# First output projection with the context's tiles first, and the context's expert products in three runs per expert

## The chip, the cores and the metric

The kernel runs on one core of one Trainium2 chip. The metric is the device time of one execution in microseconds, and times shown are medians of several executions. The engines are named as in the profile: PE (TensorE), DVE (VectorE), ACT (ScalarE), POOL (GpSimd) and SP (SyncE); 16 DMA engines move data between HBM and the chip's memories for all of them.

## The reference

Two layers on 1024 latents and 256 context tokens of 1024 features. Layer 0 mixes with a hyena convolution, layer 1 with sliding-window attention; both end in an expert-choice feed-forward (each expert picks its tokens). The context is dropped after layer 1's keys, so only layer 0 has experts on the context.

```python
D_MODEL, SEQ, CTX_LEN, N_EXPERTS, EXPERT_FF, EC_CAPACITY = 1024, 1024, 256, 16, 1024, 2

def expert_choice_ffn(h, router_w, w_gate, w_up, w_down):
    B, n, D = h.shape
    cap = EC_CAPACITY * n // N_EXPERTS            # 128 latents, 32 context tokens
    aff = jax.nn.softmax((h @ router_w).astype(F32), axis=-1)
    gate, idx = lax.top_k(jnp.swapaxes(aff, 1, 2), cap)
    xe = jax.vmap(lambda hb, ib: hb[ib])(h, idx)
    a = jnp.einsum('becd,edf->becf', xe, w_gate)
    u = jnp.einsum('becd,edf->becf', xe, w_up)
    ye = jnp.einsum('becf,efd->becd', jax.nn.silu(a) * u, w_down) * gate[..., None].astype(h.dtype)
    return jax.vmap(lambda ib, yb: jnp.zeros((n, D), h.dtype).at[ib.reshape(-1)].add(yb.reshape(-1, D)))(idx, ye)

for layer in range(2):
    ...
    lat = lat + mod_l[2] * y_l                     # y_l, y_c: the mixer's output projection
    h_l = rms_norm(lat, norm2_w[layer]) * (1.0 + mod_l[4]) + mod_l[3]
    lat = lat + mod_l[5] * expert_choice_ffn(h_l, moe_router[layer], moe_w_gate[layer], ...)
    if keep_ctx:                                   # layer 0 only
        cx = cx + mod_c[2] * y_c
        h_c = rms_norm(cx, norm2_w[layer]) * (1.0 + mod_c[4]) + mod_c[3]
        cx = cx + mod_c[5] * expert_choice_ffn(h_c, ...)
return rms_norm(lat, final_norm_w)
```

## The kernel before

The program is written with a tile framework: tiles come from pools with a fixed number of buffers, a scheduler orders the instructions of each engine by a priority that follows the order of the code (`high_priority` moves a block ahead, `issue_after` ties a block behind an instruction), and a tile's buffer is used again when all readers of the tile before have ended. All weight loads of the experts are issued by SP, whose queue is in order: a load that waits for its buffer holds up the loads behind it.

**The output projection** is the class `Mix`. Its method `stream` works on one tile of 128 tokens after the other: 48 products at L777 (each f32 product is three matmuls of high and low parts), DVE's residual and norm (L780 to L789), transposes of the normed tile (L795), the router (L799), a softmax, and one transpose of the affinities (L807) that `put_lat` (L1485) or `put_ctx` (L1488) copies into `affl` (48 x 512) or `affc` (16 x 256). In layer 0 `body` calls it for the eight latent tiles, then for the two context tiles, then issues the last eight of 24 pieces of the next layer's modulation (`a1.piece`, L66), and then searches: `route_lat` finds the 128 best latents of each expert with 16 rounds of max, index and replace on DVE (L819, L820, L822; `top_rows`), and `top_rows` on `affc` finds the 32 best context tokens in four rounds. The ids of the search start the gather of the first expert's rows (`xg`, L959, on POOL), and with it the expert stage.

**The expert stage** is `Moe.run`. An expert's weights are 12 tiles `raw` of 1 MB: (e, 0) to (e, 7) are 128 rows each of gate and up (L920, L921), (e, 8) to (e, 11) are 256 rows each of down (L923). There are nine buffers for them in layer 0, so the load of each tile waits for the release of the tile nine places earlier. Each tile is split into `whi` (ACT, L935) and `wlo` (DVE, L936), three buffers each. For the latents PE multiplies with gate and up at L981 (12 matmuls of 512 columns per `raw` tile, `gu(e, kk)`) and with down at L1039 (12 per tile). `gu(e+1, 0)` and `gu(e+1, 1)` are placed inside expert e, while the activation `g` of expert e is made and transposed (L950), so the code of expert e itself begins with `gu(e, 2)`. The result is scaled on DVE (L1053) and added to the stream in HBM by an indirect DMA (L1054, the scatter).

For the context's 32 tokens of an expert PE multiplies straight from `raw` in fp32, with four column groups of 32: `ctx_gu` (L966, 4 instructions per `raw` tile, `kk` 0 to 7) and `ctx_dn` (L973, 8 instructions per down tile). One such instruction is two records in the trace. A `raw` tile is free when ACT and DVE have split it and, in layer 0, the context's products have read it. Before the change `ctx_gu` comes in pairs of `kk`: (0, 1) at the start of expert e, (2, 3) after `gu(e, 3)`, (4, 5) after `gu(e, 5)`, (6, 7) after `gu(e+1, 0)`, and `ctx_dn` comes one down tile at a time behind the L1039 products of the tile after it. L1045 transposes the context's activation, L1059 and L1060 scale and scatter it.

## Time and profile before

| What | Before |
|---|---|
| Median of 3 runs | 3269.67 us (3264.92 to 3276.31) |
| Span of the profiled execution | 3265.9 us |
| PE busy | 3024.7 us (93%) |
| DVE busy | 2365.2 us (72%) |
| ACT busy | 1625.1 us (50%) |
| POOL busy | 554.8 us (17%) |
| DMA, bytes moved | 717.12 MB, mean 220 GB/s |
| Expert stage of layer 0, PE busy from 1224 to 2020 us | 791.12 of 796 us |
| Expert stage of layer 1, PE busy from 2670 to 3235 us | 558.94 of 565 us |

The profiled execution's own time is its span, 3265.9 us, which is 3.8 us under the median. Busy time of matmuls overlaps and its ends are modelled, so a price of a matmul is read from start to start of neighbours, not from its duration.

### The profile page before, as it was taken

How to read it: one execution, taken by the hardware profiler on the slowest of the kernel's cores; microseconds unless marked ns; L12 is line 12 of the kernel's file. 1: busy time of each engine (PE TensorE's matmuls, PEld its weight loads, DVE VectorE, ACT ScalarE, POOL GpSimd, SP SyncE). 2: the span in 40 equal slices, each digit the busy share in tenths (PEclk: the TensorE clock that was granted, in tenths of full speed). 3: DMA queues.
4: the chain of work that ended last, by engine and by line, in shares of the span. 5: the costliest groups of instructions: out<-in, count | busy, mean ns of one | idle time of the engine just before them, and what ended most of it. 6: DMA issues, size and time to landing. Idle time of an engine off the chain costs nothing. (4 is left out here: it accounts for less than half of the span.)

```text
span 3265.9 us, 43095 instructions
## 1 busy us (share of the span) xinstructions
PE 3024.7 (93%) x15902; PEld 2315.5 (71%) x15902; DVE 2365.2 (72%) x3089; ACT 1625.1 (50%) x2106; POOL 554.8 (17%) x560
## 2 busy tenths in 40 slices
PE   6888999999987969999999998998999949999995
PEld 3677888876766836666666665887887838888884
DVE  6888752389996675766766765846886579999996
ACT  5456333310003425555555554426886437777774
POOL 4663000044452121010010000000000011111110
PEclk9999999999998979999999999999999969999998
DMA  7743432176726457787787785536114359999995
GB/s 226 250 167 135 127 107 81 68 231 198 251 89 215 168 195 249 268 297 277 272 299 276 272 286 178 174 100 229 54 44 149 123 212 376 397 391 394 395 379 185
DMA packets 361652, 717.12 MB, mean 220 GB/s; under 512 B 45821, under 2 KB 201997, under 8 KB 354914
## 3 DMA queue, kind: packets, MB, share of 16 engines
q1 hardware_dynamic: 324792, 669.60, 56.8%
q0 software_dynamic: 12096, 37.75, 4.6%
q10 hardware_dynamic: 24554, 7.01, 1.0%
q8 instruction: 126, 2.06, 0.3%
q14 instruction: 84, 0.69, 0.1%
HBM read 603.64 MB, written 110.62 MB: 219 GB/s over the span
## 5 line engine op out<-in xcount | busy, mean ns | idle before, releaser
L936 DVE TENSOR_TENSOR wlo<-raw,whi 128x2048 fp32r<-128x2048 f32 x379 | 862.4, 2289 | 287.6 <-ACT whi L935 284.5
L935 ACT ACTIVATE whi<-raw 128x2048 fp32r<-128x2048 f32 x384 | 734.5, 1917 | 441.0 <-PE psA L981 226.8
L981 PE MATMUL psA<-wlo,xhi 128*128 128x512 f32 x1024 | 405.1, 396 | 0.8 <-DVE wlo L936 0.8
L981 PE MATMUL psA<-whi,xlo 128*128 128x512 f32 x1024 | 404.8, 396 | 0.0
L981 PE MATMUL psA<-whi,xhi 128*128 128x512 f32 x1024 | 387.8, 405 | 0.9 <-ACT xhi L33 0.9
L981 PEld LDWEIGHTS psA<-whi,xhi 128*128 128x128 f32 x1024 | 193.2, 189 | 84.3 <-issue 40.5
L981 PEld LDWEIGHTS psA<-wlo,xhi 128*128 128x128 f32 x1024 | 193.5, 189 | 52.0 <-issue 12.6
L981 PEld LDWEIGHTS psA<-whi,xlo 128*128 128x128 f32 x1024 | 193.1, 189 | 40.5
L1054 POOL DMA_INDIRECT lat_d<-ye,ids x32 | 77.3, 2415 | 778.4 <-DVE ye L1053 778.4
L411 PE MATMUL psA<-hThi,win_hi 128*128 128x512 f32 (+1 forms) x576 | 205.8, 358 | 0.0
L411 PE MATMUL psA<-hTlo,win_hi 128*128 128x512 f32 (+1 forms) x576 | 204.4, 355 | 1.2 <-DVE hTlo L34 1.2
L411 PE MATMUL psA<-hThi,win_lo 128*128 128x512 f32 (+1 forms) x576 | 203.9, 354 | 0.0
L1039 PE MATMUL psA<-whi,ghi 128*128 128x512 f32 x512 | 163.4, 400 | 1.1 <-ACT ghi L33 1.1
L1039 PE MATMUL psA<-wlo,ghi 128*128 128x512 f32 x512 | 160.0, 394 | 0.7 <-DVE wlo L936 0.7
L1039 PE MATMUL psA<-whi,glo 128*128 128x512 f32 x512 | 158.9, 391 | 1.2 <-DVE glo L34 1.2
L571 ACT ACTIVATE q<-psT 128x512 f32<-128x512 f32 x32 | 19.1, 597 | 266.4 <-PE psT L565 147.7
L157 PE MATMUL psT<-fleaf,tabF 128*128 128x256 f32 x512 | 125.6, 397 | 20.7 <-DVE fleaf L128 19.9
L966 PE MATMUL psC<-raw,xTc 128*32 128x512 f32 x1024 | 139.7, 599 | 0.0
L413 ACT ACTIVATE p<-psA,convw 128x512 f32<-128x512 f32 (+1 forms) x72 | 44.1, 612 | 176.4 <-PE psA L411 176.4
L777 PE MATMUL psA<-wo_hi,zhi 128*128 128x512 f32 x288 | 114.6, 402 | 15.5 <-ACT zhi L33 13.8
L157 PEld LDWEIGHTS psT<-fleaf,tabF 128*128 128x128 f32 x512 | 98.7, 199 | 41.9 <-issue 23.1
L959 POOL DMA_INDIRECT xg<-hl_d,ids x32 | 50.0, 1563 | 437.9 <-PE psT L950 387.1
(349 smaller groups left out, 6530.2 us busy)
## 6 DMA issues: line engine op xcount, KB each, us to landing
raw<-in_moe_w_gate_dram SPq DMA_DIRECT2D x256, 512.0 KB
raw<-in_moe_w_up_dram SPq DMA_DIRECT2D x256, 512.0 KB
raw<-in_moe_w_down_dram SPq DMA_DIRECT2D x128, 1024.0 KB
ada_wt<-in_ada_w_dram SPq DMA_DIRECT2D x48, 1024.0 KB
K_d<-kout SPq DMA_DIRECT2D x56, 256.0 KB
Kt<-K_d SPq DMA_DIRECT2D x112, 128.0 KB
win_raw<-in_hy_w_in_dram SPq DMA_DIRECT2D x24, 512.0 KB
lf_d<-lf SPq DMA_DIRECT2D x64, 128.0 KB
```

Source lines behind the costliest of these rows:

```text
L157: nc.tensor.matmul(ps[:, m, :], k.tabF[:, l, kin, m, :], x[:, kin, :], start=(kin == 0), stop=(kin == 1))
L411: nc.tensor.matmul(pt[:, :n], a[:, kk, :], b[:, kk, s:s + n], start=(i == 0), stop=(i == 23))
L413: nc.scalar.activation(p[:, dst:dst + n], pt[:, :n], AF.Identity, bias=cw[:, 0, c:c + 1])
L571: nc.scalar.activation(self.like(self.q), self.R[l], AF.Copy)
L777: nc.tensor.matmul(pt, a[:, kk, :], b[:, kk, hs], start=(kk == 0 and p == 0), stop=(kk == 7 and p == 2))
L935: nc.scalar.activation(whi, raw, AF.Copy)
L936: (engine or nc.vector).tensor_tensor(out=wlo, in0=raw, in1=whi.bitcast(F32), op=ALU.subtract)
L959: nc.gpsimd.indirect_dma_start(out=xg, out_offset=None, in_=h_d[0], in_offset=bass.IndirectOffsetOnAxis(ap=ids[:, e:e + 1], axis=0))
L966: nc.tensor.matmul(cgu[32 * q:32 * q + 32], xc[e // 4][:, kk, (e % 4) * 32:(e % 4) * 32 + 32], self.raw(e, kk)[:, :, q * 256:(q + 1) * 256 ...
L981: nc.tensor.matmul(acc[i], a[:, kk, :], b[:, i // 2, (i % 2) * 512:(i % 2) * 512 + 512], start=(kk == 0 and p == 0), stop=(kk == 7 and p = ...
L1039: nc.tensor.matmul(dn[i], a[:, kk, :], b[:, j, i * 512:i * 512 + 512], start=(kk == 0 and p == 0), stop=(kk == 7 and p == 2))
L1054: nc.gpsimd.indirect_dma_start(out=out_d[0], out_offset=bass.IndirectOffsetOnAxis(ap=ids[:, e:e + 1], axis=0), in_=y, in_offset=None, comp ...
```

## The change

In `body`, layer 0's `Mix` takes the context's two tiles first, then the context's search is written, then the eight latent tiles and their search, and last the eight modulation pieces. In `Moe.run` the context's products of an expert from 1 on stand in three runs: `ctx_gu` of `kk` 0 to 3 behind `gu(e, 4)`, `ctx_gu` of `kk` 4 to 7 behind `gu(e, 7)`, and all four down tiles of `ctx_dn` behind the L1039 products and the scatter. Expert 0's `ctx_gu` stands as one run ahead of its `gu`. The pools of PSUM get another rule for the waits of a reused buffer (`reuse_waits="tile"`). Comments of the code were dropped too; lines after L1015 have moved by 2 to 5 (L1039 is L1043 in the changed kernel, L1045 L1048, L1485 L1487).

```diff
@@ Moe.run
-                    nc.tensor.matmul(acc[i], a[:, kk, :], b[:, i // 2, (i % 2) * 512:(i % 2) * 512 + 512],
-                                     start=(kk == 0 and p == 0), stop=(kk == 7 and p == 2))
+                    last = nc.tensor.matmul(acc[i], a[:, kk, :], b[:, i // 2, (i % 2) * 512:(i % 2) * 512 + 512],
+                                            start=(kk == 0 and p == 0), stop=(kk == 7 and p == 2))
+            return last
...
+            cgu = k.psum.tile([128, 2, 256], F32, name="psC")
+            ctx_gu(0, cgu, range(8))
         acc = banks(4)
         for kk in range(2):
             gu(0, kk, acc, xT)
         for e in range(NE):
             nxt = gather(e + 1) if e + 1 < NE else None
-            cgu = k.psum.tile([128, 2, 256], F32, name="psC") if route_c else None
-            if route_c:
-                ctx_gu(e, cgu, (0, 1))
+            if route_c and e:
+                cgu = k.psum.tile([128, 2, 256], F32, name="psC")
             for kk in range(2, 8):
-                gu(e, kk, acc, xT)
-                if route_c and kk in (3, 5):
-                    ctx_gu(e, cgu, (kk - 1, kk))
+                last = gu(e, kk, acc, xT)
+                if route_c and e and kk == 4:
+                    with k.tc.issue_after(last.ins):
+                        ctx_gu(e, cgu, range(4))
...
+            if route_c and e:
+                with k.tc.issue_after(last.ins), k.tc.high_priority(offset=50):
+                    ctx_gu(e, cgu, range(4, 8))
...
-            if route_c:
-                ctx_gu(e, cgu, (6, 7))
...
-                if route_c:
-                    if k2 == 0:
...
-                    else:
-                        ctx_dn(e, cdn, cgT, k2 - 1)
+                if route_c and k2 == 0:
...
             if route_c:
-                ctx_dn(e, cdn, cgT, 3)
+                for k2 in range(4):
+                    ctx_dn(e, cdn, cgT, k2)
@@ Psum
-        self.pool = es.enter_context(tc.tile_pool(name=f"psum{Psum.n}", bufs=1, space=PSUM))
+        self.pool = es.enter_context(tc.tile_pool(name=f"psum{Psum.n}", bufs=1, space=PSUM, reuse_waits="tile"))
@@ body
-                      k.z2_d[:, :, :T])
+                      k.z2_d[:, :, T:])
+            mix.stream(1, 2, k.z2_d[:, :, T:], k.ctx, k.ctx_d, k.hc_d, put_ctx)
+            top_c = top_rows(k, affT[1], 32, rp, "c")
             mix.stream(0, 8, k.z2_d[:, :, :T], k.x, k.lat0_d, k.hl0_d, put_lat)
-            mix.stream(1, 2, k.z2_d[:, :, T:], k.ctx, k.ctx_d, k.hc_d, put_ctx)
+            route = route_lat(k, affT[0], rp)
             for i in range(16, 24):
                 a1.piece(i)
             rows1, cols1 = a1.rows, a1.cols
-            route = route_lat(k, affT[0], rp)
-            top_c = top_rows(k, affT[1], 32, rp, "c")
```

What the scheduler makes of it is seen in the order of each engine's instructions. The first place is PE inside expert 4 of layer 0 (`psC_10989` is the bank of its `ctx_gu`, `psC_11218` that of its `ctx_dn`; the numbered `raw` are its weight tiles in order of `kk`). Before, with the L981 and L1039 rows between left out, but for those beside the transposes of `g`:

```order
L966 MATMUL psC_10989<-raw_10807,xTc_9536 32x512 x4
L966 MATMUL psC_10989<-raw_10848,xTc_9536 32x512 x4
...
L966 MATMUL psC_10989<-raw_11000,xTc_9536 32x512 x4
L966 MATMUL psC_10989<-raw_11019,xTc_9536 32x512 x4
...
L966 MATMUL psC_10989<-raw_11101,xTc_9536 32x512
L950 MATMUL psT_11182<-ident_86,g_11144 128x128 x4
L966 MATMUL psC_10989<-raw_11101,xTc_9536 32x512 x3
L966 MATMUL psC_10989<-raw_11127,xTc_9536 32x512 x4
...
L973 MATMUL psC_11218<-raw_11223,cgT_11242 32x256 x8
...
L973 MATMUL psC_11218<-raw_11246,cgT_11242 32x256 x8
```

The same expert on PE in the changed kernel, with the same rows left out:

```order
L966 MATMUL psC_10989<-raw_10815,xTc_9536 32x512 x4
L966 MATMUL psC_10989<-raw_10848,xTc_9536 32x512 x4
L966 MATMUL psC_10989<-raw_10992,xTc_9536 32x512 x4
L966 MATMUL psC_10989<-raw_11011,xTc_9536 32x512 x4
L950 MATMUL psT_11065<-ident_86,xg_10987 128x128 x4
...
L966 MATMUL psC_10989<-raw_11030,xTc_9536 32x512 x4
L966 MATMUL psC_10989<-raw_11074,xTc_9536 32x512 x4
L966 MATMUL psC_10989<-raw_11093,xTc_9536 32x512 x4
L966 MATMUL psC_10989<-raw_11119,xTc_9536 32x512 x4
L950 MATMUL psT_11182<-ident_86,g_11152 128x128 x4
...
L973 MATMUL psC_11218<-raw_11223,cgT_11242 32x256 x8
L973 MATMUL psC_11218<-raw_11246,cgT_11242 32x256 x8
```

The last products that read a `raw` tile now stand in blocks of four tiles: where before the first two tiles were done with at the head of the expert, they are now read behind `gu(e, 4)`, and the run that the transposes of `g` cut into 1 and 7 instructions is whole. SP's loads stand in the same order in both kernels.

The second place is DVE where the latents' search begins (L819, L820 and L822 on `affl`). Before, it begins when the last latent tile's affinities are copied (L1485), among the work of the two context tiles (L780, L781, and `gb` and `sr` of the context's modulation):

```order
L1485 COPY affl<-psT 16x128
L819 MAX tkvl<-affl 48x8
L820 MAX_INDEX tkil<-tkvl,affl 48x8
L780 TENSOR_TENSOR ylat<-psA,g_9010 128x512
L822 MATCH_REPLACE affl<-tkvl,affl 48x512
L764 TENSOR_TENSOR gb<-gb,g_9010 128x1024
L819 MAX tkvl<-affl 48x8
L759 TENSOR_TENSOR sr<-sr,ylat 128x1024
L781 TENSOR_TENSOR xres<-ylat,xres 128x512
L780 TENSOR_TENSOR ylat<-psA,g_9010 128x512
```

In the changed kernel no tile follows, and the rounds stand alone, but for rows of the modulation and one split of a weight tile (L936) further down:

```order
L1487 COPY affl<-psT 16x128
L819 MAX tkvl<-affl 48x8
L820 MAX_INDEX tkil<-tkvl,affl 48x8
L822 MATCH_REPLACE affl<-tkvl,affl 48x512
L819 MAX tkvl<-affl 48x8
...
L819 MAX tkvl<-affl 48x8
L936 TENSOR_TENSOR wlo<-raw,whi 128x2048
L820 MAX_INDEX tkil<-tkvl,affl 48x8
```

The search moved from beside the last two tiles to behind the last tile. Layer 1 has the same order of instructions in both kernels on every engine.

## Rows read from the trace of the kernel before

**Rows 1.** Busy time of each engine in the two expert stages (window in us; its length; busy us and count of PE, PE's weight loads, DVE, ACT, POOL; PE's granted clock, 1.00 being 2.4 GHz; DMA share; GB/s).

```profile
1224.00:2020.00 796.00, 791.12 (x4672) 514.03 (x4672) 522.75 (x349) 423.99 (x326) 69.87 (x49) 1.00 0.75 268
2670.00:3235.00 565.00, 558.94 (x2560) 457.47 (x2560) 505.38 (x317) 410.09 (x286) 80.51 (x31) 1.00 0.94 357
```

**Rows 2.** The transposes L1045, one pair per expert, from expert 1 to expert 14 of layer 0 (duration ns min/median/max, first and last start us).

```profile
L1045 PE MATMUL psT<-ident,cg x28: 272/272/273, 1326.0 to 1962.5; 128*128 128x128 f32 x28
```

**Rows 3.** The chain that ended last, in layer 1's expert stage, which has no context (start us, us, what).

```profile
2702.71 10.88 PE psA L1039 x48
...
2727.68 0.44 PE psT L950 x4
2728.12 4.55 PE psA L981 x20
...
2737.42 10.88 PE psA L1039 x48
```

**Rows 4.** PE's timeline in layer 0 around a run of two `kk` (start us, us, engine line op out<-in xcount).

```profile
1501.24 0.39 PE L981 MATMUL psA<-whi,xlo 128*128 128x512 f32 x1
1501.56 1.92 PE L966 MATMUL psC<-raw,xTc 128*32 128x512 f32 x16
1503.41 0.50 PE L981 MATMUL psA<-whi,xhi 128*128 128x512 f32 x1
1503.75 0.40 PE L981 MATMUL psA<-wlo,xhi 128*128 128x512 f32 x1
```

**Rows 5.** PE's timeline a little later in the same expert, around the run that the transposes of `g` cut.

```profile
1511.98 0.39 PE L981 MATMUL psA<-whi,xlo 128*128 128x512 f32 x1
1512.30 1.05 PE L966 MATMUL psC<-raw,xTc 128*32 128x512 f32 x2
1513.28 0.66 PE L950 MATMUL psT<-ident,g 128*128 128x128 f32 x4
1513.87 1.92 PE L966 MATMUL psC<-raw,xTc 128*32 128x512 f32 x14
...
1516.05 0.40 PE L981 MATMUL psA<-wlo,xhi 128*128 128x512 f32 x1
```

**Rows 6.** PE's timeline at the end of expert 0, around the context's products of the last two down tiles (x32).

```profile
1286.44 0.63 PE L1039 MATMUL psA<-whi,glo 128*128 128x512 f32 x2
1287.00 1.93 PE L973 MATMUL psC<-raw,cgT 128*32 128x256 f32 x32
...
1289.20 0.40 PE L981 MATMUL psA<-wlo,xhi 128*128 128x512 f32 x1
```

**Rows 7.** What ACT waited for in its splits in layer 0's expert stage (engine line, waited for: us in total, times, longest us).

```profile
ACT whi L935 <- DMA raw<-in_moe_w_up_dram: 55.8, 15, 9.8
```

**Rows 8.** ACT's timeline in expert 1: splits that waited for a weight tile to land (in brackets the idle time before, and what ended it).

```profile
1303.62 1.91 ACT L935 ACTIVATE whi<-raw 128x2048 fp32r<-128x2048 f32 x1 [9.75 <-DMA raw<-in_moe_w_up_dram]
...
1306.18 3.72 ACT L935 ACTIVATE whi<-raw 128x2048 fp32r<-128x2048 f32 x2 [0.17 <-DMA raw<-in_moe_w_up_dram]
```

**Rows 9.** PE's timeline behind the first of these two splits.

```profile
1307.91 0.50 PE L981 MATMUL psA<-wlo,xhi 128*128 128x512 f32 x1 [0.83 <-DVE wlo L936]
```

**Rows 10.** SP's issues of weight tiles around the scatters at the end of expert 3 (each tile is a gate and an up half; the gate halves are shown), and the scatter's issue on POOL.

```profile
1436.08 0.33 SPq L920 DMA_DIRECT2D raw<-in_moe_w_gate_dram  x1
...
1441.97 0.33 SPq L920 DMA_DIRECT2D raw<-in_moe_w_gate_dram  x1
...
1436.93 1.57 POOL L1054 DMA_INDIRECT lat_d<-ye,ids  x1 [25.95 <-DVE ye L1053]
```

**Rows 11.** ACT's timeline: the split of the tile whose gate half was issued at 1441.97.

```profile
1451.48 1.91 ACT L935 ACTIVATE whi<-raw 128x2048 fp32r<-128x2048 f32 x1 [4.86 <-DMA raw<-in_moe_w_up_dram]
```

**Rows 12.** DMA queues from 1344 to 1351 us, while the scatters of expert 1 run (queue, kind: packets, MB, share of 16 engines; q1 carries the weight loads, q0 the scatters).

```profile
q1 hardware_dynamic: 392, 1.42, 54.1%
q0 software_dynamic: 280, 0.65, 49.1%
```

**Rows 13.** Busy time of each engine while PE idles once in the hyena stage, and right after (columns as in rows 1).

```profile
907.55:911.27 3.72, 0.01 (x1) 0.00 (x1) 3.72 (x5) 0.00 (x0) 3.72 (x2) 0.92 0.14 41
911.27:914.68 3.41, 3.41 (x9) 2.77 (x10) 3.41 (x5) 0.00 (x0) 2.93 (x4) 0.58 0.86 277
```

**Rows 14.** Timelines at the end of layer 0's projection: DVE at the last latent tile, PE's last product of a tile, the first and the last step of the latents' search, and PE's first transpose of gathered rows.

```profile
1133.34 0.69 DVE L780 TENSOR_TENSOR ylat<-psA,g 128x512 f32<-128x512 f32 x1 [2.91 <-PE psA L777]
...
1147.16 0.28 DVE L1485 COPY affl<-psT 16x128 f32<-16x128 f32 x1 [1.67 <-PE psT L807]
...
1163.25 0.39 PE L777 MATMUL psA<-wo_hi,zlo 128*128 128x512 f32 x1
...
1212.19 0.67 DVE L820 FIND_INDEX8 tkil<-tkvl,affl 48x8 uint32<-48x512 f32 x1
...
1216.52 1.14 POOL L959 DMA_INDIRECT xg<-hl_d,ids  x1 [12.05 <-issue]
...
1224.23 1.09 PE L950 MATMUL psT<-ident,xg 128*128 128x128 f32 x4 [2.53 <-DMA xg<-hl_d,ids]
```

**Rows 15.** The same search and gather in layer 1, where nothing stands between, from the chain that ended last (start us, us, what).

```profile
2627.05 0.70 DVE tkvl L819
...
2662.13 0.76 DVE tkil L820 x2
...
2665.87 4.25 DMA xg<-hl_d,ids
```

More of the change, by code (lines that the diff above doesn't have):

```diff
@@ L28 @@
 class K:
+    pass
 def split(nc, hi, lo, src):
@@ L1040, in run @@
                                              start=(kk == 0 and p == 0), stop=(kk == 7 and p == 2))
-                if route_c:
-                    if k2 == 0:
-                        pt = k.psum.tile([128, 4, 128], F32, name="psT")
-                        for j in range(2):
-                            nc.tensor.transpose(pt[:, j, :], cg[:, j * 128:(j + 1) * 128], k.ident)
-                        cgT = pool.tile([128, 2, 128], F32, name="cgT", bufs=2)
-                        nc.scalar.activation(cgT, pt[:, 0:2, :], AF.Copy)
-                    else:
-                        ctx_dn(e, cdn, cgT, k2 - 1)
+                if route_c and k2 == 0:
+                    pt = k.psum.tile([128, 4, 128], F32, name="psT")
+                    for j in range(2):
+                        nc.tensor.transpose(pt[:, j, :], cg[:, j * 128:(j + 1) * 128], k.ident)
+                    cgT = pool.tile([128, 2, 128], F32, name="cgT", bufs=2)
+                    nc.scalar.activation(cgT, pt[:, 0:2, :], AF.Copy)
             y = pool.tile([128, D], F32, name="ye", bufs=1)
```

## Prediction

> **What bounds the kernel now.** I read the busy times by stage first. In layer 0's expert stage PE is busy 791 of 796 us at the full clock, with the 16 DMA engines at 0.75 and DVE and ACT far below [rows 1]; layer 1's stage is as full. So in the stage that the change rewrites PE's work sets the pace, and a microsecond less of PE's work is a microsecond less of time, as long as the weights come. The period of an expert is read from L1045: 14 pairs from 1326.0 to 1962.5 us are 13 periods, 48.96 us each [rows 2]. Layer 1, the same products without a context, has 34.71 us from one block of L1039 to the next [rows 3]. The difference, 14.25 us per expert, is what the context costs on PE.
>
> It can be taken apart on PE's timeline. L981 follow each other every 0.2275 us (20 in 4.55) [rows 3]. Between the L981 at 1501.24 and the one after next at 1503.75 lie 2.51 us, of which two steps are L981's own: a run of two `kk` costs 2.05 us [rows 4]. The run cut by the transposes takes 1511.98 to 1516.05, 4.07 us; without two steps of L981 and 0.44 us for the four transposes [rows 3] it costs 3.17 [rows 5]. Two down tiles cost 2.07 us (from 1286.44 + 0.46 for its pair to 1289.20 - 0.23) [rows 6]. A record of L966 takes about 0.107 us in the long run: 16 records then are 1.71 and each run has a fixed 0.34 for the change from one column layout to the other and back. So one down tile alone is (2.07 - 0.34) / 2 + 0.34 = 1.2. The sum is 3 x 2.05 + 3.17 + 2 x 1.2 + 2.07 + 0.33 (L1045) = 14.1, as measured.
>
> Next I asked who waits for weights. ACT's splits waited 55.8 us for weights to land, in 15 places of up to 9.8 us [rows 7]; PE felt almost nothing of it: once, in expert 1, it stood 0.83 us [rows 9]. The supply has a small reserve, not a large one.
>
> **The products' three runs.** A run of four `kk` is 32 records, 32 x 0.107 + 0.34 = 3.76 us, and the four down tiles are 4 x 0.865 + 0.34 = 3.8. Three such runs and L1045 are 11.65, so PE's work of an expert is 34.71 + 11.65 = 46.36 us, 2.6 us less than now. Experts 1 to 14 give 36.4; the last, whose `ctx_dn` now lies behind its own scatter, about 4.2, together 40.6. Expert 0's `ctx_gu` is one run of 64 records, 7.2 us instead of 9.3, and its `ctx_dn` gives 0.7: 2.8 us, less a little for transposes and gathers that cut the run; I take 2.5. The gain of PE's work is 43 us.
>
> **What the longer runs hold back.** A `raw` tile comes free when its last reader ends, and SP's queue is in order. Take time from t0, the end of an expert's `ctx_dn`, where `gu(e, 2)` starts. Now two tiles come free some 5 us into the expert and two more after each pair; after the change four come free in the run of `ctx_dn` (batch A), four in the run behind `gu(e, 4)` (batch B), four behind `gu(e, 7)`. With nine buffers and 12 tiles per expert, the tiles that take the place of batch A are (e, 5), (e, 6) and, by e modulo 3, either (e, 7) or not. Where e is 2 modulo 3, (e, 7) is in A; where e is 0, it is the first of B; where e is 1, the second of B; in expert 1 even (1, 6) is the first of B.
>
> When PE wants (e, 7): 36 L981 (8.19), the run (3.76), transposes (0.44), 24 L981 (5.46), transposes (0.44): t0 + 18.3. When it can have it: the first tile of A is free one down tile after the run's start, t0 - 2.45. An idle queue takes about 5 us to the first tile; after that a full queue brings 413 GB/s at most, 2.54 us per tile and in expert 1 a tile's split could start 2.56 us after that of the tile before, when it landed [rows 8]. But just then the scatters run. Of the tile issued at 1441.97, the third from 1436.08, the split started at 1451.48 [rows 10, 11]: 9.5 us from its issue and 15.4 from the first, where 5 us from an issue to an idle queue would be 1446.9: 4.5 us late. So A's last tile lands at t0 - 2.45 + 5 + 3 x 2.55 + 4.5 = 14.7. Batch B is issued by t0 + 9.4 (8.19 + 0.34 + 0.86), waits behind A, and its first lands at 17.25, its second at 19.8. From landing to use go 4.3 us, `whi` and `wlo` (from 1303.6, where the split starts, to 1307.91, where PE goes on) [rows 8, 9]. PE's stall at `gu(e, 7)` is therefore 0 for e of 2 modulo 3; 17.25 + 4.3 - 18.3 = 3.25 for e of 0 modulo 3; 5.8 for e of 1; and about 6.4 in expert 1, whose `gu(1, 6)` waits. Experts 3, 6, 9, 12, 15 give 16.3, experts 4, 7, 10, 13 give 23.2: with expert 1 a total of **46 us**. Bounds: were the loads not held up by the scatters, B's first tile would land one idle-queue latency after its issue, at 14.3, and the stalls would be 0.3, 2.8 and about 3: 16 us. Taking the 15.4 us of the three tiles whole and 2.55 for a fourth, A ends at 15.5 and the stalls are 4, 6.6 and 7: 53. I take the middle value, since rows 10 are nearest in place: the same scatter at the same distance from the load.
>
> How far the scatter holds the loads up is the price that decides. In 7 us of a scatter the weight queue moved 1.42 MB [rows 12] where 413 GB/s would have moved 2.89: 3.5 us lost by bytes, against 4.5 by the landing. The Trainium skill (DMA: Bandwidth & Descriptors, section Queues, rings and completion order) says that each DMA engine takes turns between the queues that have work, a packet at a time; the two shares of rows 12, 54% and 49%, agree. By even turns alone the loads would lose half of the 7 us, 3.5, each stall would be 1 us shorter, and the sum about 10 us lower.
>
> **The order of the projection.** PE's last product ends at 1163.5 [rows 14]. Now the latents' search runs beside the last two tiles; after the change it begins behind the last tile. One more tile's transposes and router (about 3) and a short wait for the first latent tile stand ahead of the last product, so it ends near 1167.5. From there to the copy of the affinities it took 13.8 us (1133.34 to 1147.16): 1181.3. The search alone takes 35.9 us (2627.05 to 2662.90 in layer 1) [rows 15], and a weight split of 2.29 and the modulation's rows stand in it: it ends near 1220.4, now 1212.9 [rows 14]: 7.5 later. The gather behind it now takes 7.7 us (1216.52 to 1224.23), because the first weight tiles land at the same time; in layer 1 it took 4.25 [rows 15]. With the pool of the projection free from about 1181, the weights land before, and I take 3.4 back. The expert stage starts **4 us later**; 0 if the last tile's chain is shorter without a tile behind it, 10 if the gather stays slow. The context's search of four rounds is hidden among the latent tiles, where DVE idles 2.9 us per tile [rows 14]. The pools' other waits change boundaries of stages: 0, within 1 us either way.
>
> **Sum.** -43 + 46 + 4 = +7 on the profiled execution's 3265.9: 3273 us. That execution is 3.8 us under the median, so the median to expect is **3277 us**. About 0.3%, 9.8 us, is what a measurement of this kernel can tell from no change; +7 is within it.
>
> **Rivals.**
> 1. *The loads stay hidden.* If the scatter costs the loads little, the stalls are 16 us or less: -43 + 16 + 4 = -23, 3247; with none, 3231. For it speaks that PE waited just once so far [rows 9] and that the DMA engines have a quarter of their time free [rows 1]; against it rows 7 and 10. It turns at an excess of 0.7 us less than I take: then the sum is 0.
> 2. *PE's clock falls in the stalls.* After an idle time of 3.7 us PE ran for 3.41 us at 0.58, between its two levels of 1.2 and 2.4 GHz and mostly at the lower [rows 13]. That cost 3.41 x 0.42 = 1.4 us, and twice that if it stayed as long again. The stalls of experts 1, 4, 7, 10, 13 are of 5 to 6 us, in two pieces (for `whi`, then 2.3 us for `wlo`); with 1.4 to 3 us each, 7 to 15 more: 3284 to 3292, slower; with the upper bound of the stalls on top, 3299. Against it: no idle time in two close pieces stands in the rows. The Trainium skill (TensorE: Matmul & The Clock Gate, section Why this matters for your kernels) says that idle gaps of PE between matmuls bring the lower clock back; rows 13 agree.
> 3. *The search is the larger loss.* If the gather is as slow as now and the last chain no shorter, the stage starts 10 us later: 3283, the rest as forecast.
>
> **Chances.** The forecast (stalls of 35 to 50 us, small clock losses, 3265 to 3282) 0.42; rival 1 0.27; rival 2 0.23; rival 3 0.08. The faster part is nearly all rival 1: 0.27. The slower part is rivals 2 and 3 and a little of the forecast's upper end: 0.36. The rest, 0.37, is within 0.3%. The range from 3246 (rival 1 with its stalls of 16) to 3300 (rival 2 with the longer stalls) leaves out rival 1 without any stall and worse than rival 2, about 2 in 10. The forecast's own range is 3265 to 3284.
>
> **What would show it.** Right: L1045 to L1045 comes to 46.4 us where e is 2 modulo 3 and some 49.5 and 52 in the other two, in a cycle of three; PE idles before L981 of the eighth tile, released by `wlo` and, behind it, by the weights' landing; the sum of that idle time is 35 to 50 us. The search's last step ends near 1220 and the first L981 of the stage starts some 4 us later than now. Wrong: even periods of 46.4 (rival 1), or rows of the stage with PE's granted clock under 1 behind the stalls (rival 2), or periods above 52 that come from something else, such as a run of 32 records that is dearer than 3.76.

## The result: slower by 0.9%, by the mechanism that was forecast and with three terms off

The changed kernel takes 3302.57 us (3295.63 to 3306.2, 4 runs) against 3268.59 us before (4 runs beside it). The ratio estimated from the runs is 1.0093, 95% interval 1.0078 to 1.0109; the two medians alone give 1.0104. The time is 25.6 us over the forecast of 3277 and 2.6 us over the top of its range; as a ratio it lies at that top (3300 to 3269.67 is 1.0093). Of the cases it is rival 2, with a worse projection. The profiled execution has a span of 3304.1 us. One run of the third kernel below (3307.49 us) was slower throughout, at a lower clock: that kernel's median of 3238.45 us counts it (3237.75 without it), its ratio does not.

The page of the profile after, first section and the two wait groups of L981 in section 5 (columns as in the notes on the page: busy us and share; for a group, busy us, mean ns, idle time before and its releaser):

```profile
span 3304.1 us, 43091 instructions
...
PE 3012.0 (91%) x15902; PEld 2340.2 (71%) x15902; DVE 2366.1 (72%) x3089; ACT 1625.1 (49%) x2104; POOL 582.0 (18%) x560
...
L981 PE MATMUL psA<-wlo,xhi 128*128 128x512 f32 x1024 | 410.2, 401 | 6.4 <-DVE wlo L936 6.4
L981 PE MATMUL psA<-whi,xhi 128*128 128x512 f32 x1024 | 383.2, 406 | 28.9 <-ACT whi L935 28.1
```

PE is busy 13 us less than before and the kernel is longer: PE now waits 34.5 us in front of L981 for `whi` (28.1) and `wlo` (6.4), where it had waited 0.8 us [rows 9].

The transposes of `cg` of experts 2 to 5 in the changed kernel (PE's timeline; they answer to [rows 2]):

```profile
1392.96 0.38 PE L1048 MATMUL psT<-ident,cg 128*128 128x128 f32 x2
...
1443.22 0.38 PE L1048 MATMUL psT<-ident,cg 128*128 128x128 f32 x2
...
1497.34 0.38 PE L1048 MATMUL psT<-ident,cg 128*128 128x128 f32 x2
...
1543.51 0.38 PE L1048 MATMUL psT<-ident,cg 128*128 128x128 f32 x2
```

The periods are 50.3, 54.1 and 46.2 us for experts 3, 4 and 5, and so they go on in a cycle of three; before, each was 48.96. Experts 2, 5 and 8 have become 2.8 us shorter, experts 11 and 14 1.8 and 1.6; expert 6 is as long as before (48.8), and the others are longer.

Why expert 4 has 54.1 is seen in SP's, ACT's and PE's timelines of it:

```profile
1464.89 0.38 SPq L923 DMA_DIRECT2D raw<-in_moe_w_down_dram  x1
1465.74 0.33 SPq L920 DMA_DIRECT2D raw<-in_moe_w_gate_dram  x1
...
1476.59 1.91 ACT L935 ACTIVATE whi<-raw 128x2048 fp32r<-128x2048 f32 x1 [7.96 <-DMA raw<-in_moe_w_up_dram]
...
1473.31 0.60 PE L950 MATMUL psT<-ident,xg 128*128 128x128 f32 x4
1478.55 2.08 PE L981 MATMUL psA<-whi,xhi 128*128 128x512 f32 x4 [4.64 <-ACT whi L935]
...
1484.81 3.64 PE L966 MATMUL psC<-raw,xTc 128*32 128x512 f32 x32
```

At 1464.89 SP issues the first tile of batch B, (4, 8), at 1465.74 the second, (4, 7). The second lands some 11 us later, behind batch A; ACT, which had waited 8 us for it, splits it at 1476.59, and PE, done with `gu(4, 6)` and its transposes at 1473.9, idles 4.64 us. From 1473.9 to the run of the context at 1484.81 go 10.9 us for 12 matmuls that need 2.73. PE's clock in these stretches (columns as in [rows 1]):

```profile
1473.90:1478.55 4.65, 0.01 (x2) 0.00 (x1) 0.02 (x1) 1.96 (x2) 1.00 (x1) 0.91 1.03 414
1478.55:1482.00 3.45, 3.24 (x7) 2.14 (x8) 3.45 (x3) 3.45 (x3) 0.00 (x0) 0.50 0.80 315
1482.00:1485.40 3.40, 3.40 (x16) 2.14 (x18) 2.72 (x3) 2.20 (x4) 0.00 (x0) 0.63 0.01 2
```

Behind the idle time the granted clock is 0.50, the lower level of 1.2 GHz, and mostly so in the next stretch. Of the 8 us that this expert loses against the 46.2 of expert 5, some 6 are the weights and 2 the clock; the working stands in the part on the prediction.

The next larger part of the loss lies ahead of the experts. PE's and DVE's timelines around layer 0's projection, answering to [rows 14]:

```profile
1084.51 1.94 PE L795 MATMUL psT<-ident,ylat 128*128 128x128 f32 x8 [5.52 <-DVE ylat L789]
...
1174.16 0.48 PE L777 MATMUL psA<-wo_hi,zlo 128*128 128x512 f32 x1
1174.57 1.92 PE L66 MATMUL psD<-ada_wt,sc 128*32 128x512 f32 x16
1181.70 1.91 PE L66 MATMUL psD<-ada_wt,sc 128*32 128x512 f32 x2 [5.21 <-DMA ada_wt<-in_ada_w_dram]
1183.55 1.97 PE L795 MATMUL psT<-ident,ylat 128*128 128x128 f32 x8
1185.45 1.93 PE L66 MATMUL psD<-ada_wt,sc 128*32 128x512 f32 x6
1187.31 2.08 PE L799 MATMUL psT<-router,h2T 128*128 128x16 f32 x16
...
1190.92 0.28 DVE L1487 COPY affl<-psT 16x128 f32<-16x128 f32 x1 [0.46 <-PE psT L807]
...
1230.56 0.68 DVE L820 FIND_INDEX8 tkil<-tkvl,affl 48x8 uint32<-48x512 f32 x1
...
1240.91 0.50 PE L981 MATMUL psA<-whi,xhi 128*128 128x512 f32 x1 [0.75 <-ACT xhi L33]
```

And the clock of the 14 us in which the latents' first tiles run (columns as in [rows 1]):

```profile
1082.00:1096.00 14.00, 11.49 (x40) 10.15 (x41) 8.63 (x21) 4.60 (x9) 2.35 (x1) 0.52 0.41 141
```

The last product ends at 1174.4 in place of 1163.5. Of these 11 us 2 lie ahead of the first product (1011.9, before 1009.8) and 9 between the first and the last: 162.3 us in place of 153.4. There PE waits 5.5 us for the first latent tile's norm, and its clock is at 0.50 from 1081.8 to 1095.4. Before, PE's wait at that boundary, of 4.57 us, came at the first context tile (1170.0), behind the last product. The last tile's way from there to its affinities takes 16.3 us: modulation pieces (L66) that wait for their own weights stand ahead of its transposes and of its router on PE. Then comes the search, alone. The expert stage begins at 1240.9; before, at 1226.0.

### The profile page after: what moved, and what is told of

The parts are those of the page before. It is cut to its first block, busy times and chain, and to the rows that moved or that the text cites. A ratio compares the mean times of both kernels' runs of the same rounds, so it can differ in the third digit from the quotient of the medians.

```text
span 3304.1 us, 43091 instructions
## 1 busy us (share of the span) xinstructions
PE 3012.0 (91%) x15902; PEld 2340.2 (71%) x15902; DVE 2366.1 (72%) x3089; ACT 1625.1 (49%) x2104; POOL 582.0 (18%) x560
## 4 chain that ended last, share of the span: by engine, by line
PE 56%; issue 24%; DVE 8%; DMA 5%; POOL 4%; ACT 2%; SPq 0%; ACTq 0%; DVEq 0%; POOLq 0%
PE psA L981 11%; PE psA L411 10%; PE psA L1043 5%; PE psA L1125 4%; PE psA L777 4%; PE psA L157 3%; PE psT L157 2%; PE psT L1269 2%; DMA lat_d<-ye,ids 2%; PE psT L558 1%; PE psT L565 1%; PE psA L1263 1%; PE psD L66 1%; PE psS L1243 1%; PE psA L1264 1%
## 5 line engine op out<-in xcount | busy, mean ns | idle before, releaser
L936 DVE TENSOR_TENSOR wlo<-raw,whi 128x2048 fp32r<-128x2048 f32 x379 | 862.1, 2289 | 260.4 <-ACT whi L935 257.1
L981 PE MATMUL psA<-wlo,xhi 128*128 128x512 f32 x1024 | 410.2, 401 | 6.4 <-DVE wlo L936 6.4
L981 PE MATMUL psA<-whi,xlo 128*128 128x512 f32 x1024 | 409.9, 401 | 0.0
L981 PE MATMUL psA<-whi,xhi 128*128 128x512 f32 x1024 | 383.2, 406 | 28.9 <-ACT whi L935 28.1
L981 PEld LDWEIGHTS psA<-whi,xhi 128*128 128x128 f32 x1024 | 194.9, 191 | 79.7 <-ACT whi L935 33.5
L1055 POOL DMA_INDIRECT lat_d<-ye,ids x32 | 104.2, 3258 | 817.6 <-DVE ye L1054 817.6
L981 PEld LDWEIGHTS psA<-wlo,xhi 128*128 128x128 f32 x1024 | 197.3, 193 | 50.2 <-DVE wlo L936 11.5
L981 PEld LDWEIGHTS psA<-whi,xlo 128*128 128x128 f32 x1024 | 197.1, 193 | 41.0
L1043 PE MATMUL psA<-whi,ghi 128*128 128x512 f32 x512 | 159.9, 393 | 1.1 <-ACT ghi L33 1.1
L1043 PE MATMUL psA<-wlo,ghi 128*128 128x512 f32 x512 | 160.2, 394 | 0.7 <-DVE wlo L936 0.7
L1043 PE MATMUL psA<-whi,glo 128*128 128x512 f32 x512 | 158.6, 391 | 1.2 <-DVE glo L34 1.2
L1245 DVE CUSTOM_DVE_ANT_0 P<-psS,band,sink 128x640 f32<-128x640 f32 (+1 forms) x128 | 107.4, 846 | 21.1 <-PE psS L1243 20.3
```

What stands on the lines that cost most here:

```text
L936: (engine or nc.vector).tensor_tensor(out=wlo, in0=raw, in1=whi.bitcast(F32), op=ALU.subtract)
L981: last = nc.tensor.matmul(acc[i], a[:, kk, :], b[:, i // 2, (i % 2) * 512:(i % 2) * 512 + 512], start=(kk == 0 and p == 0), stop=(kk == 7 ...
L1043: nc.tensor.matmul(dn[i], a[:, kk, :], b[:, j, i * 512:i * 512 + 512], start=(kk == 0 and p == 0), stop=(kk == 7 and p == 2))
L1055: nc.gpsimd.indirect_dma_start(out=out_d[0], out_offset=bass.IndirectOffsetOnAxis(ap=ids[:, e:e + 1], axis=0), in_=y, in_offset=None, comp ...
L1245: V.tensor_tensor_reduce(out=P[:, r, :nk], in0=S[:, 256:256 + nk], in1=masks[b], scale=-0.125, scalar=sink[:, h:h + 1], op0=ALU.add, op1=A ...
```

## Experiments

The runs below stand beside runs of the kernel before on the same chip, whose median there is given.

**The two parts, each alone.** The first kernel is the changed one with the projection of before:

```diff
-                      k.z2_d[:, :, T:])
-            mix.stream(1, 2, k.z2_d[:, :, T:], k.ctx, k.ctx_d, k.hc_d, put_ctx)
-            top_c = top_rows(k, affT[1], 32, rp, "c")
+                      k.z2_d[:, :, :T])
             mix.stream(0, 8, k.z2_d[:, :, :T], k.x, k.lat0_d, k.hl0_d, put_lat)
-            route = route_lat(k, affT[0], rp)
+            mix.stream(1, 2, k.z2_d[:, :, T:], k.ctx, k.ctx_d, k.hc_d, put_ctx)
             for i in range(16, 24):
                 a1.piece(i)
             rows1, cols1 = a1.rows, a1.cols
+            route = route_lat(k, affT[0], rp)
+            top_c = top_rows(k, affT[1], 32, rp, "c")
```

> The changed kernel with the projection of before: the expert stage with its three runs, and PSUM's rule, alone. Theory (the two parts add up; late weights at gu(e, 7) and the clock behind them cost more than the runs save): L1048 of expert 0 to L1048 of expert 15 some 747 us as in the changed kernel, 18 us more than before, so 18 to 21 us over before, about 3288. Rival (the expert stage is slow only because the projection starts it 15 us late, with its loads elsewhere): within 8 us of before.

Measured: 3292.58 us against 3270.63, ratio 1.0069 (1.0053 to 1.0086), 22 us. From expert 0's transpose to expert 15's:

```profile
L1048 PE MATMUL psT<-ident,cg x32: 270/272/273, 1278.2 to 2022.5; 128*128 128x128 f32 x32
```

That is 744 us, where 747 were expected, and in the kernel before 729 (second of the next fences). So the three runs with their stalls cost 15 us on experts 1 to 15. The rest of the 22 us fits expert 0, which is read from its first product, since this execution was the kernel's fastest (3283.46 us) and its projection, in the order of before, ended 5.4 us earlier than in the profile of before. Four fences show expert 0: the first matmul of `gu(0, 0)` and the transposes of `cg` in the kernel before, then that first matmul in this kernel, and what PE waited for there from 1215 to 1297 us (us, times, longest):

```profile
1226.00 0.79 PE L981 MATMUL psA<-whi,xhi 128*128 128x512 f32 x1 [0.69 <-ACT xhi L33]
```

```profile
L1045 PE MATMUL psT<-ident,cg x32: 272/272/329, 1277.8 to 2006.6; 128*128 128x128 f32 x32
```

```profile
1220.15 0.79 PE L981 MATMUL psA<-whi,xhi 128*128 128x512 f32 x1 [0.75 <-ACT xhi L33]
```

```profile
PE psT L894 <- DMA xg<-hc_d,cid: 4.8, 2, 4.3
```

Before: 1226.0 to 1277.8, 51.8 us. Here: 1220.2 to 1278.2, 58.0. All but the first 15 of its latents' products now stand behind expert 0's context products, and these need the four gathers of context rows (L888), which share two buffers with the latents' gathers; PE waits 4.8 us for them, with nothing else it may do, and behind the longer of the two waits its clock is at 0.50 (1240.9 to 1246.6 us).

The second kernel is the one of before, with its PSUM rule, and the projection of the change (the same lines the other way).

> The kernel before with the projection and searches of the change alone. Theory: the first L981 of the expert stage comes 15 us later, at about 1241, and the experts keep their 48.96 us: 14 to 16 us over before, about 3284. Rival (as the prediction had it, 4 us later): 3270 to 3274.

Measured: 3280.72 us against 3270.63, ratio 1.0033 (1.0020 to 1.0045), 10 us. Its first L981:

```profile
1233.01 0.50 PE L981 MATMUL psA<-whi,xhi 128*128 128x512 f32 x1 [0.69 <-ACT xhi L33]
```

The stage starts 7 us later than before, not 15, and the experts keep their 48.95 us. Of the 8 us to the changed kernel's profile, 4 lie ahead of the first product:

```profile
1007.72 0.80 PE L777 MATMUL psA<-wo_hi,zhi 128*128 128x512 f32 x1 [10.48 <-ACT zhi L33]
```

```profile
1011.87 0.80 PE L777 MATMUL psA<-wo_hi,zhi 128*128 128x512 f32 x1 [12.14 <-ACT zhi L33]
```

The first line is this kernel's, the second the changed kernel's. Another 2.4 us lie between the first and the last product (159.9 us here, 162.3 there). PE waits 5.5 us for the first latent tile here too, but its clock comes back sooner: the same window from 1082 to 1096 us has 0.89,

```profile
1082.00:1096.00 14.00, 13.64 (x78) 11.47 (x76) 7.27 (x20) 4.99 (x12) 4.75 (x2) 0.89 0.42 148
```

where the changed kernel had 0.52. The other PSUM rule is not needed for that: the seventh kernel below, without it, was at 0.50 as long as the changed one, from 1074.4 to 1088.1 us. The rest lies behind the last product. One profile of each is thin ground here: with the projection in the order of before, the first product of the experts came between 1220.2 and 1230.8 us in seven profiled executions (1224.8 in the mean), with that of the change at 1240.9, 1233.0 and, in the fourth kernel below, 1238.0.

22 and 10 us are 32 of the 34 that both parts cost together: the parts add up, neither needs the other.

**The slot of the late tile.** The layer's nine buffers lie in two pools, of two and of seven, and a tile's pool was fixed by its number modulo nine. The third kernel deals the tiles from the tenth on to the pools in the order in which buffers come free; else it is the first one.

```diff
-        self.loaded, self.split = {}, {}
+        self.loaded, self.split, self.slot = {}, {}, {}
...
-            pool, bufs = self.pools[len(self.loaded) % len(self.pools)]
+            n = len(self.loaded)
+            if self.layer == 0 and n >= 9:
+                slot = self.slot[divmod(n - 9, 12)]
+            else:
+                slot = n % len(self.pools)
+            self.slot[e, i] = slot
+            pool, bufs = self.pools[slot]
```

> As the kernel with the expert stage of the change and the projection of before, but the weight tiles from the tenth on are dealt to the two pools in the order in which their buffers come free, so that (e, 7) gets a buffer of the down tiles in every expert, and not one that the run behind gu(e, 4) frees. Nothing else changes. Theory (the stall is the slot of (e, 7), not the length of the runs): every expert has the 46.2 us that experts 2, 5 and 8 have now, no PE wait for whi or wlo over 1 us from expert 2 on, 57 us under the kernel with the slots as they were, about 3231, 38 under before. Rival (four tiles at once are too much for the DMA engines whatever slot they have): within 15 us of the kernel with the slots as they were.

Measured: 3238.45 us against 3270.63, ratio 0.9890 (0.9868 to 0.9911), 32 us less than before and 54 less than the kernel with the slots as they were. The transposes:

```profile
L1054 PE MATMUL psT<-ident,cg x32: 270/272/273, 1288.7 to 1975.1; 128*128 128x128 f32 x32
```

From 1288.7 to 1975.1 go 686.4 us; the periods of experts 2 to 14 are 46.2 to 47.0. The wait for `whi` and `wlo` is gone from the list of PE's waits in this stage, whose longest is

```profile
PE psA L1049 <- ACT ghi L33: 0.7, 1, 0.7
```

Four loads at once are not too much; a late slot for one of them is. The expected 3231 was missed by 7 us: it was 57 us under a first kernel taken at 3288, and the first kernel came out at 3292.6 and the difference at 54. Expert 0 still costs its 58 us.

**The same dealing without the runs.** The tenth kernel is the one of before with the same lines for the slots.

> The kernel before with the weight tiles dealt to the two pools in the order in which their buffers come free, as in the kernel with the slots dealt, and its eight runs of the context's products kept. Theory (dealing the slots gives nothing by itself, since PE does not wait for weights there; it lets the longer runs pay): periods of 48.9 us, within 0.3% of before. Rival (the gain of the kernel with the slots dealt comes from the dealing, not from the three runs): 20 us or more under before.

Measured: 3272.44 us against 3271.65, ratio 1.0004 (0.9993 to 1.0015).

```profile
L1051 PE MATMUL psT<-ident,cg x32: 272/272/330, 1275.2 to 2002.9; 128*128 128x128 f32 x32
```

727.7 us, as before. The dealing is worth nothing where PE does not wait; it is the runs that give the 42 us from expert 0's transpose to expert 15's (728.8 to 686.4), and the dealing that lets them.

**The scatters.** The fourth kernel is the changed one without the two scatters of each expert of layer 0.

```diff
-            nc.gpsimd.indirect_dma_start(out=out_d[0], out_offset=bass.IndirectOffsetOnAxis(ap=ids[:, e:e + 1], axis=0),
+            if not route_c:
+              nc.gpsimd.indirect_dma_start(out=out_d[0], out_offset=bass.IndirectOffsetOnAxis(ap=ids[:, e:e + 1], axis=0),
                                          in_=y, in_offset=None, compute_op=ALU.add)
...
-                nc.gpsimd.indirect_dma_start(out=ctx_rows,
-                                             out_offset=bass.IndirectOffsetOnAxis(ap=cids[:, e:e + 1], axis=0),
-                                             in_=yc, in_offset=None, compute_op=ALU.add)
+                pass
```

> The changed kernel without the two indirect scatters of each expert in layer 0 (L1055 and L1062 left out, so the experts add nothing to the streams of layer 0). Theory (the scatters hold up the four loads of the first batch by some 4.5 us): the stall in front of gu(e, 7) falls to under 1 us where e is 0 modulo 3 and to about 2.5 us where it is 1, periods 46.2, 46.5 and 49, no half clock behind them: 30 to 40 us under the changed kernel, 3262 to 3272. Rival (the loads are late by their own latency and order, not by the scatters): less than 10 us.

Measured: 3262.47 us against 3270.63, ratio 0.9977 (0.9966 to 0.9989), 40 us under the changed kernel. PE's waits from 1300 to 2045 us, and the transposes:

```profile
PE psA L981 <- ACT whi L935: 11.2, 10, 2.1
PE psA L981 <- DVE wlo L936: 3.5, 4, 1.1
```

```profile
L1048 PE MATMUL psT<-ident,cg x32: 270/272/273, 1295.9 to 2006.9; 128*128 128x128 f32 x32
```

34.5 us of waits have become 14.7, and 747 us from expert 0's transpose to expert 15's have become 711: 36 of the 42 us between the two profiled executions, the rest lies behind the experts. Experts 3, 6 and 9 have 46.5, 46.2 and 46.6, as expected, expert 12 47.5; experts 4, 7, 10 and 13 have 51.5, 50.6, 48.6 and 48.7, two of them more than the 49 that was expected. In these two the clock fell, against the expectation: PE was at 0.50 for 3.4 us in expert 4 (from 1472.4 us) and in expert 7 (from 1615.7), and at 1.00 throughout in experts 10 and 13. So the scatters hold up the loads, and they are the larger part of the stall; 24 us over the 686.4 of the dealt slots remain without them, the late slots' part with the clock behind it.

**Expert 0.** The fifth kernel is the third with expert 0's products where the other experts have them.

```diff
-            cgu = k.psum.tile([128, 2, 256], F32, name="psC")
-            ctx_gu(0, cgu, range(8))
...
-            if route_c and e:
+            if route_c:
                 cgu = k.psum.tile([128, 2, 256], F32, name="psC")
...
-                if route_c and e and kk == 4:
+                if route_c and kk == 4:
...
-            if route_c and e:
+            if route_c:
                 with k.tc.issue_after(last.ins), k.tc.high_priority(offset=50):
```

> The kernel with the slots dealt by release and the projection of before, with expert 0's context products no longer ahead of its gu but in two runs behind gu(0, 4) and gu(0, 7), as the other experts have them. Theory (expert 0 loses because its context products wait for four gathers of context rows, L888, ahead of its latents' products): from the first matmul of gu(0, 0) to expert 0's transpose of cg 50 us in place of 58, about 8 us under the kernel with the slots dealt, 3231. Rival (the gathers are waited for wherever the products stand): within 3 us of it.

Measured: 3227.42 us against 3273.10, ratio 0.9876 (0.9855 to 0.9896): 46 us less than before, and the fastest of all. The first matmul (L987 is L981 in this kernel) and the transposes:

```profile
1220.25 0.79 PE L987 MATMUL psA<-whi,xhi 128*128 128x512 f32 x1 [0.75 <-ACT xhi L33]
```

```profile
L1052 PE MATMUL psT<-ident,cg x32: 270/272/273, 1268.4 to 1957.1; 128*128 128x128 f32 x32
```

Expert 0 takes 48.2 us, where 50 were expected: 9.8 less than with its products ahead and 3.6 less than before.

**The projection.** Two kernels vary the second one. In the sixth the modulation's pieces are written between the context's tiles and the latents':

```diff
             top_c = top_rows(k, affT[1], 32, rp, "c")
+            for i in range(16, 24):
+                a1.piece(i)
             mix.stream(0, 8, k.z2_d[:, :, :T], k.x, k.lat0_d, k.hl0_d, put_lat)
             route = route_lat(k, affT[0], rp)
-            for i in range(16, 24):
-                a1.piece(i)
```

> The experts of before with the projection of the change, but the eight pieces of modulation (L66) written between the context's tiles and the latents', not behind the search. Theory (the pieces' matmuls, which wait for their weights, stand on PE ahead of the last latent tile's transposes and router): from the last L777 to the last copy of latent affinities 14 us in place of 16.5, and 2 to 3 us under the kernel with the change's projection, 3278. Rival (the pieces wait for their weights wherever they stand, now ahead of more tiles): 3283 or more.

Measured: 3288.86 us against 3273.10, ratio 1.0058 (1.0040 to 1.0076): the rival. PE's timeline:

```profile
1059.67 1.92 PE L66 MATMUL psD<-ada_wt,sc 128*32 128x512 f32 x16
1062.98 0.50 PE L777 MATMUL psA<-wo_hi,zhi 128*128 128x512 f32 x1 [1.39 <-ACT zhi L33]
...
1178.02 0.48 PE L777 MATMUL psA<-wo_hi,zlo 128*128 128x512 f32 x1
```

The last tile's way to its affinities did fall, from 16.5 to 14.5 us (1178.0 to 1192.5). But the first latent tile's products begin at 1063.0, behind all the pieces, and the last one ends at 1178 in place of 1167.6. The pieces cost less behind the tiles than ahead of them.

In the seventh the context's search is written behind the latents':

```diff
-            top_c = top_rows(k, affT[1], 32, rp, "c")
             mix.stream(0, 8, k.z2_d[:, :, :T], k.x, k.lat0_d, k.hl0_d, put_lat)
             route = route_lat(k, affT[0], rp)
+            top_c = top_rows(k, affT[1], 32, rp, "c")
```

> The experts of before with the projection of the change, but the context's search written behind the latents' search. Theory (PE's idle time and half clock at the first latent tile come from the new modulation and the residual's addition on POOL, not from the search's steps on DVE): PE still idles some 5 us before the transposes of the first latent tile, and the four rounds of the context, some 4.5 us, come on top of the latents' search: 3280 to 3286. Rival (the context's search between the tiles makes the first latent tile late): PE's idle time there goes, 3274 or less.

Measured: 3280.85 us against 3273.10, ratio 1.0029 (1.0014 to 1.0045), as the second kernel. PE's wait at the first latent tile is still there:

```profile
1076.82 1.09 PE L795 MATMUL psT<-ident,ylat 128*128 128x128 f32 x4 [6.36 <-DVE ylat L789]
```

So the context's search on DVE does not cause it. That it is the new modulation and POOL's addition to the residual (L771), which the same boundary of streams had before at the context's tiles, fits the timelines, but no run took these away: the cause of this wait stays open.

**The PSUM rule.** The eighth kernel changes that line alone.

> The kernel before with nothing but the other rule for waits of reused PSUM buffers. Theory (it changes a few waits at the boundaries of stages): within 0.3% of before. Rival (it costs or gives part of what is left over between the two parts): 5 us or more either way.

Measured: 3274.99 us against 3273.10, ratio 1.0011 (1.0000 to 1.0021): within 0.3%.

**The clock.** The ninth kernel is the first with twenty matmuls of zeros, added into a bank of the same sum, between `gu(e, 6)` and `gu(e, 7)` of five experts (`zz` is a tile of zeros; for its room `cg` has one buffer in place of two).

```diff
+                if route_c and kk == 6 and e in (1, 4, 7, 10, 13):
+                    with k.tc.issue_after(last.ins), k.tc.high_priority(offset=100):
+                        for i in range(20):
+                            nc.tensor.matmul(acc[0], zz, xT[0][:, 0:4, :].rearrange("p a b -> p (a b)"),
+                                             start=False, stop=False)
```

> The expert stage of the change with the projection of before, and in experts 1, 4, 7, 10 and 13 twenty more matmuls ahead of gu(e, 7), or ahead of the place where PE waits for it: zeros times the latents, added to the same bank, 4.6 us of PE's time in which it would idle. Theory (about 2 us of each of these stalls are the half clock behind the idle time): PE's granted clock stays 1.00 behind these stalls, the periods of experts 4, 7, 10 and 13 fall from 54 to 52 us, 7 to 10 us less in all, about 3284. Rival (the clock costs nothing there, the weights are late all the same): periods of 54 us or more, 3292 or more.

Measured: 3303.83 us against 3271.65, ratio 1.0103 (1.0081 to 1.0124): 11 us over the first kernel, the rival's side. Expert 1's stall lies ahead of `gu(1, 6)`, so there the matmuls came on top of it (period 56.5 in place of 52.4). In expert 4 they filled the longer part of the wait; PE behind them, and its clock (columns as in [rows 1]):

```profile
1463.51 4.74 PE L1019 MATMUL psA<-xhi,zz 128*128 128x512 f32 x20
...
1468.74 0.51 PE L981 MATMUL psA<-whi,xhi 128*128 128x512 f32 x1
1471.07 0.50 PE L981 MATMUL psA<-wlo,xhi 128*128 128x512 f32 x1 [1.82 <-DVE wlo L936]
```

```profile
1463.50:1468.30 4.80, 4.80 (x23) 3.92 (x22) 0.00 (x0) 1.53 (x1) 0.00 (x0) 1.00 1.03 412
1468.30:1471.07 2.77, 0.89 (x6) 0.33 (x4) 2.35 (x2) 2.77 (x3) 2.11 (x1) 1.00 0.51 204
1471.07:1474.50 3.43, 3.43 (x9) 2.71 (x10) 3.43 (x3) 2.68 (x4) 0.82 (x1) 0.60 0.51 146
```

The clock stayed at 1.00 through the zeros and fell behind the short wait for `wlo`, so the period is 54.7 as without them. Experts 7 and 13 went the same way (54.6 and 54.9). In expert 10 the wait behind the zeros was 1.52 us, and the clock stayed at 1.00 throughout:

```profile
1734.40:1787.20 52.80, 51.12 (x311) 36.02 (x310) 32.72 (x23) 26.57 (x20) 7.23 (x3) 1.00 0.74 263
```

Its period is 52.9. So in the same kernel a fall of the clock for 3.4 us (1471.8 to 1475.2 in expert 4) goes with 1.7 to 2 us more, of which 0.3 to 0.5 are longer waits, near the theory's 2; the zeros kept the clock up in one expert of four, and there they brought 0.8 us against the first kernel's 53.7.

## Why the prediction missed, step by step

**The gain of PE's work: right.** 2.6 us per expert were forecast, 40.6 from expert 1 on. Where nothing is late, the experts have 46.16 us, 2.8 less than before, and with the dealt slots experts 1 to 15 give 42.4.

**The late tile: right in its place, order and cause.** A cycle of three, the stall ahead of `gu(e, 7)`, ahead of `gu(1, 6)` in expert 1, nothing in experts 2, 5 and 8 (1.0 and 1.2 us in 11 and 14); the scatter as the larger cause; the wait behind a landing, though `whi` released 28.1 of the 34.5 us and not `wlo`. Forecast periods of 49.6 and 52.2 are 48.8 to 50.4 and 53.7 to 54.4 in the changed kernel. **Its size was too small**: 46 us were summed, and over the dealt slots experts 1 to 15 lose 61 (747.1 - 686.4). The stall itself was sized about right: PE's waits add up to 34.5 us, just under the 35 to 50 that were named. What the sum lacked is mostly the clock: experts 4, 7, 10 and 13 lose 8.4 us more than forecast. Expert 4 is the case: PE is ready at 1473.9, and `wlo` follows `whi` (at 1478.5) by about 2.3 us, at 1480.8; at the full clock the eight matmuls left then end by 1482.7, 6.0 us late, where 5.8 was forecast. It was 1484.81, so 2.1 us are the clock's. The half clock was priced as rival 2 at 1.4 to 3 us in each of five experts with a chance of 0.23. It came in all five, for 6.8 us each as in expert 4 (1477.7 to 1484.6 us), in expert 15 too, and for 3.4 us in experts 3 and 9, but not in 6 and 12. It should have stood in the sum: the stalls forecast for the five experts, 5.8 and 6.4 us, were longer than the 3.7 us of [rows 13] behind which the clock was seen to fall. Expert 15 lost 6.6 in place of 3.3.

**The dispute over the scatter's price.** It was 4.5 us by the landing against 3.5 by bytes. The even turns of the queues that the Trainium skill states (DMA: Bandwidth & Descriptors, section Queues, rings and completion order) would give the lower price. Without the scatters the stalls are 24.5 us in place of 60.7: 36 us over the ten experts that stall, 3.6 each with the clock's part in it. But where e is 0 modulo 3 hardly any stall was left, so more could not be saved there; in experts 4, 7, 10 and 13 the saving was 2.7, 3.8, 5.5 and 5.0. The runs do not decide between the two prices.

**Expert 0: the wrong sign.** A gain of 2.5 us was forecast, from fewer records; the first kernel shows a loss of 6.2 (51.8 to 58.0), and the changed kernel 2.5 (1240.9 to 1295.2, 54.3). Against the second kernel, which has the same projection and expert 0 as before (1233.0 to 1282.4, 49.4), the changed kernel's loss is 4.9. The step that failed is the half-sentence "less a little for transposes and gathers that cut the run". Four gathers through two buffers stand in front of that run, and before, `gu(0, 0)` and `gu(0, 1)` covered them: PE had waited 0.4 us for them, and in the first kernel waits 4.8 and then runs at the lower clock. The fifth kernel, without that run in front, takes 48.2.

**The projection: 4 us forecast, 7 in the second kernel's profile and 15 in the changed kernel's.** The search alone (39 us; 40.0 measured from 1191.2 to 1231.2) and the quicker gather behind it (3.4 back; from 1234.89 to 1239.54 it took 4.65 in place of 7.7) were right. The last tile's chain was taken at 13.8 us, from a tile that no modulation pieces disturb; with L66 ahead of its transposes and its router it is 16.3 to 16.5. In the kernel before the pieces already stood on PE behind the last product (the first at 1163.6 us), and I priced the search behind them and not the tile. The end of the last product was forecast at 1167.5, 4 us later. The second kernel's 1167.9 agrees by luck: its products began 2.1 us earlier than before and took 6.5 us more. In the changed kernel they took 8.9 more and ended at 1174.4. The step that failed is "a short wait for the first latent tile", about 1 of the 4 us: it was 5.5 us in both kernels, with the lower clock behind it (to 1085.0 us in the second kernel, to 1095.4 in the changed one). I had costed that boundary by PE's work and not by its idle time. Rival 3's stage start of 10 us later does not follow from the forecast's own terms either, where a slow gather gives 7.5.

**Sum.** In the two profiled executions, before and changed: +14.9 up to the first L981, +2.5 in expert 0, +18.3 in experts 1 to 15 (747.1 against 728.8), and 2.5 behind: 38.2. Forecast: +4, -2.5, +5.4. The top of the range, 3300, had the longer stalls and the clock in it, but the projection at 4 us only and expert 0 as a gain; cases of both kinds came together.

## What to carry to other kernels

Grouping work that frees buffers makes the releases lumpy: before counting the work saved, follow the one load whose buffer is freed last and ask when its reader comes. Where buffers lie in more than one pool, deal the tiles by the order of release and not by number: here that turned a loss of 22 us into a gain of 32, and it costs nothing. An idle time of the engine that sets the pace is to be priced with the slower clock that may follow it, in the sum and not only as a rival.

## What the runs showed of the hardware

PE's clock fell behind a wait of only 1.82 us for `wlo` in the ninth kernel, in a stretch of 2.77 us in which PE was busy 0.89: the next 3.43 us were granted 0.60, although PE had run without a gap and at 1.00 for the 4.80 us before that stretch. In expert 10 of the same execution it stayed at 1.00 behind zeros and a wait of 1.52 us. Filling the longer part of a wait with useless matmuls is therefore no safe way to keep the clock.

Two almost equal pairs of waits in one execution of the changed kernel ended differently: 0.69 and 1.33 us in expert 3, and 0.78 and 1.36 us in expert 6. Behind the second wait of each pair PE was granted 0.52 and 1.00:

```profile
1426.70:1430.10 3.40, 3.40 (x8) 2.70 (x9) 2.66 (x2) 2.06 (x5) 0.00 (x0) 0.52 0.98 392
1577.30:1580.70 3.40, 3.40 (x21) 2.02 (x25) 3.14 (x3) 2.86 (x5) 0.00 (x0) 1.00 0.92 365
```

So a term that depends on the clock behind an idle time has a spread of its own: a fall for 3.4 us cost some 1.5 us in the ninth kernel, and it did not come each time.
